# Moving the short convolution of a hybrid decoder block from the attention stage to the gate stage, by way of DRAM

## The chip, the cores and the metric

One Trainium2 chip; the kernel runs on one NeuronCore of it. The metric is the device time of one execution in microseconds. Engines are named as in the profile: PE is TensorE (matmul), PEld its weight loads, DVE is VectorE, ACT is ScalarE, POOL is GpSimd, SP is SyncE, which here issues nearly all DMAs. Each engine works through its own queue in order.

## The reference

One decoder block in float32: 1024 tokens and 16 meta tokens, 1024 channels. The part that matters is the mixer: one input projection gives eight groups of 1024 channels; a short gated convolution and a stick-breaking attention run on them side by side, and two sigmoid gates merge the two.

```python
def hybrid_mixer(xn, w_in, conv_w_mix, w_proj_conv, w_proj_attn, b_gate, w_out):
    h = xn @ w_in
    b_c, c_c, h_c, q, k, v, g_conv, g_attn = jnp.split(h, list(splits), axis=-1)
    y_conv = b_c * causal_dwconv(c_c * h_c, conv_w_mix)      # 3 taps, per channel
    branch_conv = y_conv @ w_proj_conv
    o = stick_breaking_attention(q.reshape(hd), k.reshape(hd), v.reshape(hd))
    branch_attn = o.reshape(bsz, seq_len, D_ATTN) @ w_proj_attn
    gate_conv = jax.nn.sigmoid(g_conv + b_gate[0])
    gate_attn = jax.nn.sigmoid(g_attn + b_gate[1])
    merged = gate_conv * branch_conv + gate_attn * branch_attn
    return merged @ w_out
```

After it come a residual with RMSNorm, a gated MLP with a convolution of its own, and a second residual.

## The kernel before

Activations lie transposed, channels on the 128 partitions and positions along the free axis. 1026 positions are worked on (`NQ`), in three chunks of 342 (`CH`). To keep float32 precision, each operand of a product is split into a high and a low part of type float32r: ScalarE casts the high part, VectorE (or GpSimd, for weights) subtracts it from the value to get the low part. The helper `split` does this (L64, L65). Each product is then three matmuls: high by high, high by low, low by high (L124 to L126).

**Dense items.** A list of items holds the input projection, one item for each block of 128 output channels. An item is three chunks of 24 matmuls each (8 blocks of input channels, three matmuls each) into one of three PSUM buffers (`ps_mm`), and after each chunk a function of the item, `evac`, takes the result out of PSUM. The class `Dense` runs them step by step, one step being three matmuls; `chunk()` runs eight steps. At an item's start the weights of the next are split (`whi` by ScalarE, `wlo` by GpSimd, 2 buffers each) and those of the one after are loaded (`raw`, 2 buffers, L100).

**Attention stage.** For 8 pairs of heads, two streams of attention work, `stage1` (scores, sigmoids, a scan along the keys on VectorE, products on GpSimd) and `stage2` (transposes into PSUM, split into `ah` and `al`, products with the values), are interleaved with dense steps by a planner that weighs costs written in the code. For each pair the dense items are: v, q and k of the next pair, the three items of one convolution block (`items_conv`: c, h and b) and one gate (four with the last pair). The convolution block works so: `evac_c` copies c out of PSUM (ScalarE, L272), `evac_h` multiplies it by h (VectorE, L276), and after the third chunk of h `conv3` runs on the whole block of 1026 positions: one tap on ScalarE (L196), two on VectorE (L197, L198). `evac_b` multiplies by b (VectorE, L283), and the result goes to the DRAM tensor `y_d` (L285). The tiles of this work (`cc`, `yy`, the gates' `gt`, `vt`, `ot`) share four buffers of the tag `wk`.

**Gate stage.** When the attention work is through, the gate items that are left run alone on TensorE. The buffers of the attention stage are given up and reused: `yT` (three tiles, one for each chunk of positions, high and low) lies there, and the pool `sw` with two buffers a tag. In this loop `load_split` loads a block of `y_d` into `ld` (L553) and splits it into `yT`; it is called once ahead of each of the first eight chunks.

**After it.** `item_pc` multiplies `yT` by `w_proj_conv` (8 items; each chunk reads all eight blocks of `yT`), takes in the gate `gcl` (L594) and stores `m_d`; meanwhile `o_d` is split into `oT`. `item_pa` does the same for attention and adds the two (L615). Then come the output projection, the norms and the MLP.

The framework puts the instructions of each engine into an order of its own, from the program's order as priority and its own estimate of when an instruction can start; so a load or a cast can stand ahead of instructions that the program names earlier. Semaphores are placed by it too.

Of the kernel before, what the change touches and what calls it, by code (L numbers as in the profile page):

```python
# [8 lines left out]
F32 = mybir.dt.float32  # L9
F32R = mybir.dt.float32r  # L10
AF = mybir.ActivationFunctionType
ALU = mybir.AluOpType
PSUM = bass.MemoryType.PSUM

P = 128
D = 1024
KB = D // P
NMETA = 16
T0 = 14
NT = 1040  # L20
NQ = NT - T0
CH = NQ // 3
# [10 lines left out]
def block_kernel(ctx, tc, x, meta_tokens, g_pre_mix, w_in, channels, w_proj_conv,  # L33
                 w_proj_attn, w_out, g_post_mix, g_pre_ffn, w_up_gate, w_down,
                 g_post_ffn, out):
    nc = tc.nc

    def pool(name, bufs=1, side="left", space=None):
        kw = dict(name=name, bufs=bufs, reuse_waits="tile")
        if space is not None:  # L40
            kw["space"] = space
        else:
            kw["side"] = side
        return tc.tile_pool(**kw)
# [6 lines left out]
    par = const.tile([P, 106], F32, name="par")  # L51

    o_d = tc.dram_tile([D, NQ], F32, name="o_d")
    y_d = tc.dram_tile([D, NQ], F32, name="y_d")
    gc_d = tc.dram_tile([D, NQ], F32, name="gc_d")
    ga_d = tc.dram_tile([D, NQ], F32, name="ga_d")
    m_d = tc.dram_tile([D, NQ], F32, name="m_d")
# [5 lines left out]
    def split(hi, lo, src, lo_engine=None):  # L63
        nc.scalar.copy(hi, src)  # L64
        (lo_engine or nc.vector).tensor_tensor(lo, src, hi.bitcast(F32), op=ALU.subtract)  # L65
# [89 lines left out]
    def col_block(w, c):  # L155
        return w[c]
# [28 lines left out]
    work = at_ctx.enter_context(pool("work", 2, "right"))  # L185
    def w_mix(k, b):
        return par[:, k * 8 + b:k * 8 + b + 1]
# [7 lines left out]
    def conv3(dst, src, n, wt):  # L195
        nc.scalar.activation(dst, src[:, 2:2 + n], AF.Copy, scale=wt(2))  # L196
        nc.vector.scalar_tensor_tensor(dst, src[:, 1:1 + n], wt(1), dst, op0=ALU.mult, op1=ALU.add)  # L197
        nc.vector.scalar_tensor_tensor(dst, src[:, 0:n], wt(0), dst, op0=ALU.mult, op1=ALU.add)  # L198
# [67 lines left out]
    def items_conv(cb):  # L266
        st = {}

        def evac_c(ci, a, n, ps):
            if ci == 0:  # L270
                st["c"] = work.tile([P, NT], F32, name="cc", tag="wk", bufs=4)
            nc.scalar.copy(st["c"][:, a - 12:a - 12 + n], ps)  # L272

        def evac_h(ci, a, n, ps):
            c = st["c"][:, a - 12:a - 12 + n]
            nc.vector.tensor_tensor(c, c, ps, op=ALU.mult)  # L276
            if ci == 2:
                st["y"] = work.tile([P, NT], F32, name="yy", tag="wk", bufs=4)
                conv3(st["y"][:, :NQ], st["c"], NQ, lambda k: w_mix(k, cb))

        def evac_b(ci, a, n, ps):
            y = st["y"][:, a - T0:a - T0 + n]
            nc.vector.tensor_tensor(y, y, ps, op=ALU.mult)  # L283
            if ci == 2:
                nc.sync.dma_start(y_d[cb * P:(cb + 1) * P, :], st["y"][:, :NQ])  # L285

        return [(col_block(w_in, 8 + cb), src_x, CH_C, evac_c),
                (col_block(w_in, 16 + cb), src_x, CH_C, evac_h),
                (col_block(w_in, cb), src_x, CH_Q, evac_b)]
# [121 lines left out]
    n_gates = len(items)  # L411
    dense = Dense(ps_mm, items)
# [132 lines left out]
    sw = s_ctx.enter_context(pool("sw", 2, "right"))  # L545
    gp["p"], gp["n"] = sw, 2

    def slot_tile(pl, name):
        return pl.tile([P, 2, KB, CH], F32R, name=name, tag="t")

    def load_split(tiles, src_d, kb):
        raw = sw.tile([P, NT], F32, name="ld", tag="ld")
        nc.sync.dma_start(raw[:, :NQ], src_d[kb * P:(kb + 1) * P, :])  # L553
        for c in range(3):
            split(tiles[c][:, 0, kb, :], tiles[c][:, 1, kb, :], raw[:, c * CH:(c + 1) * CH])

    yT = [slot_tile(pl, "yT") for pl in (slotA, slotB, slotC)]
    k = 0
    for _ in range(3 * (n_gates - dense.i)):
        if k < 8:  # L560
            load_split(yT, y_d, k)
            k += 1
        dense.chunk()
    while k < 8:
        load_split(yT, y_d, k)
        k += 1

    xnt_ctx.close()
# [60 lines left out]
    k = 0  # L629
# [67 lines left out]
    def out_products(b, c):  # L697
        n = min(CH, D - c * CH)
        ps = ps_o.tile([P, 512], F32, name="po", tag="po")[:QB, :n]
        m = mb[b]  # L700
        for kb in range(KB):
            mh, ml = m[:, 0, kb, :], m[:, 1, kb, :]
            wh, wl = w_o[c][:, 0, kb, :n], w_o[c][:, 1, kb, :n]
            nc.tensor.matmul(ps, mh, wh, start=(kb == 0), stop=False)
            nc.tensor.matmul(ps, ml, wh, start=False, stop=False)
            nc.tensor.matmul(ps, mh, wl, start=False, stop=(kb == KB - 1))
        return ps
# [253 lines left out]
    for b in range(9):  # L961
# [3 lines left out]
        for c in range(3):  # L965
            ps = out_products(b, c)
# [156 lines left out]
    for gi, fbs in enumerate(groups):  # L1123
# [14 lines left out]
        for tb in range(8):  # L1138
# [3 lines left out]
            for hf in range(2):  # L1142
                ps = bank()
                c = slice(hf * 512, (hf + 1) * 512)
# [6 lines left out]
                a = accs[tb][:, c]  # L1151
# [10 lines left out]
            if last:  # L1162
                a, hb, s0 = accs[tb], hbs[tb], ssqs[tb]
                nc.vector.tensor_tensor(s0[:, 0:1], s0[:, 0:1], s0[:, 1:2], op=ALU.add)
                r = rstd_of(fsml, s0[:, 0:1], P)
                for hf in range(2):
                    c = slice(hf * 512, (hf + 1) * 512)
# [60 lines left out]
```

## Time and profile before

| what | value |
|---|---|
| median of 3 runs | 2078.82 us (2075.2 to 2084.7) |
| the profiled execution's own time | 2078.02 us |
| its span in the profile | 2076.3 us |
| TensorE busy | 1990.4 us (96%) |
| VectorE busy | 1069.5 us (52%) |
| ScalarE busy | 850.8 us (41%) |
| GpSimd busy | 902.0 us (43%) |
| DMA | 177.58 MB, mean 86 GB/s |

The attention stage lasts until about 1012 us of the span (its last value product starts at 1011.24), the gate stage until 1058 us, the projections until about 1250 us; the rest is the output projection, the norms and the MLP. Matmul durations overlap each other in the trace, so the pace of TensorE is read from start to start. A row of the timeline gives the start, the duration, the engine, the line and the tiles, and in brackets how long the engine was idle before it and what ended that.

### The profile page before, as it was taken

Reading aid. Unit: us, or ns where it says so; the run is one execution under the profiler, and the core shown is the slowest. Engines: PE = TensorE matmul, PEld = TensorE weight load, DVE = VectorE, ACT = ScalarE, POOL = GpSimd, SP = SyncE. Lnnn points to the kernel's source line nnn. Section 1 sums busy time; section 2 is a strip of 40 time slices with the busy share of each in tenths; the row PEclk is TensorE's granted clock in tenths of the full one; section 3 lists DMA queues with packets and bytes.
Section 4 is the critical chain, followed back from the end, with each engine's and each line's share of the span. In section 5 each row is a group of like instructions: output and inputs, shape, how many; then the busy total and the mean of one; then the engine's idle time right before and its main releaser. Section 6 shows DMA issues by size and latency. Waiting matters only on the chain.

```text
span 2076.3 us, 30859 instructions
## 1 busy us (share of the span) xinstructions
PE 1990.4 (96%) x12228; PEld 1862.1 (90%) x12228; DVE 1069.5 (52%) x1689; ACT 850.8 (41%) x1771; POOL 902.0 (43%) x764
## 2 busy tenths in 40 slices
PE   5999999999999999999999989979999999999997
PEld 5999999999999999999999989968898899878886
DVE  6455565655555565654341115785444444445546
ACT  4444454545454454544341113354334434421122
POOL 4343444434443444444222551225655556555353
PEclk9999999999999999999999999989999999999999
DMA  3111101111111101111475664313222122253323
GB/s 134 42 51 42 61 32 51 42 51 41 52 51 42 52 31 54 49 42 61 141 225 173 177 193 136 96 44 102 76 88 82 62 102 70 74 182 103 100 81 132
DMA packets 56030, 177.58 MB, mean 86 GB/s; under 512 B 12728, under 2 KB 12728, under 8 KB 55884
## 3 DMA queue, kind: packets, MB, share of 16 engines
q1 hardware_dynamic: 54732, 173.50, 25.9%
q8 instruction: 96, 1.57, 0.3%
q10 hardware_dynamic: 1152, 2.10, 0.3%
q14 instruction: 50, 0.41, 0.1%
HBM read 131.36 MB, written 44.21 MB: 85 GB/s over the span
## 4 chain that ended last, share of the span: by engine, by line
PE 78%; DVE 9%; DMA 4%; ACT 3%; POOL 2%; issue 2%; DVEq 0%; SPq 0%; ACTq 0%; POOLq 0%
PE mm L124 13%; PE mm L125 12%; PE mm L126 12%; PE st L858 6%; PE st L862 6%; PE st L860 6%; PE st L1150 3%; PE tp L372 3%; PE st L1148 3%; PE st L1149 3%; PE av L362 2%; PE av L363 2%; PE z L326 2%; PE z L325 2%; POOL a_op L65 1%
## 5 line engine op out<-in xcount | busy, mean ns | idle before, releaser
L124 PE MATMUL mm<-xnT,whi 128*128 128x342 f32 (+2 forms) x1536 | 506.9, 330 | 3.6 <-ACT xnT L64 3.6
L125 PE MATMUL mm<-xnT,whi 128*128 128x342 f32 (+2 forms) x1536 | 495.0, 322 | 0.5 <-DVE xnT L65 0.5
L126 PE MATMUL mm<-xnT,wlo 128*128 128x342 f32 (+2 forms) x1536 | 492.0, 320 | 0.0
L338 POOL TENSOR_TENSOR be<-be,fl 114x127 f32<-114x127 f32 (+2 forms) x144 | 176.8, 1228 | 402.7 <-DVE fl L336 185.8
L124 PEld LDWEIGHTS mm<-xnT,whi 128*128 128x128 f32 x1536 | 291.0, 190 | 8.4 <-ACT xnT L64 4.2
L125 PEld LDWEIGHTS mm<-xnT,whi 128*128 128x128 f32 x1536 | 291.5, 190 | 2.2 <-DVE xnT L65 1.0
L126 PEld LDWEIGHTS mm<-xnT,wlo 128*128 128x128 f32 x1536 | 290.6, 189 | 0.0
L65 POOL TENSOR_TENSOR wlo<-raw,whi 128x1024 fp32r<-128x1024 f32 x80 | 205.7, 2572 | 188.0 <-ACT whi L64 188.0
L65 POOL TENSOR_TENSOR a_op<-raw,a_op 128x512 fp32r<-128x512 f32 (+1 forms) x136 | 191.7, 1422 | 94.4 <-ACT a_op L64 74.1
L336 DVE TENSOR_TENSOR_SCAN fl<-fl 114x128 f32<-114x128 f32 (+2 forms) x144 | 204.9, 1423 | 4.9
L65 DVE TENSOR_TENSOR al<-tp,ah 128x342 fp32r<-128x342 f32 (+4 forms) x288 | 127.0, 450 | 139.5 <-ACT ah L64 137.3
L64 ACT CAST ah<-tp 128x342 fp32r<-128x342 f32 (+4 forms) x288 | 112.8, 398 | 189.8 <-PE tp L372 181.5
L858 PE MATMUL st<-opT,a_op 128*128 128x258 f32 (+2 forms) x528 | 173.1, 328 | 3.4 <-ACT snap L873 1.7
L860 PE MATMUL st<-opT,a_op 128*128 128x258 f32 (+2 forms) x528 | 170.6, 323 | 1.7 <-DVE opT L65 1.7
L862 PE MATMUL st<-opT,a_op 128*128 128x258 f32 (+2 forms) x528 | 170.4, 323 | 0.0
L327 ACT ACTIVATE fl<-z 114x348 f32<-114x348 f32 (+10 forms) x240 | 111.4, 464 | 129.8 <-PE z L326 122.5
L64 ACT CAST a_op<-raw 128x512 fp32r<-128x512 f32 (+1 forms) x136 | 85.0, 633 | 152.4 <-DMA raw<-in_w_up_gate_dram 50.4
L1155 DVE TENSOR_TENSOR acc<-acc,st 128x512 f32<-128x512 f32 x144 | 98.5, 687 | 91.2 <-PE st L1150 91.2
L372 PE MATMUL tp<-ident,be 114*128 114x114 f32 x720 | 119.5, 263 | 25.5 <-DVE al L65 21.1
L858 PE MATMUL st<-opB,a_op 128*128 128x512 f32 (+2 forms) x396 | 127.9, 323 | 0.0
L860 PE MATMUL st<-opB,a_op 128*128 128x512 f32 (+2 forms) x396 | 127.8, 323 | 0.0
L862 PE MATMUL st<-opB,a_op 128*128 128x512 f32 (+2 forms) x396 | 127.3, 322 | 0.0
(172 smaller groups left out, 4367.3 us busy)
## 6 DMA issues: line engine op xcount, KB each, us to landing
raw<-in_w_in_dram SPq DMA_DIRECT2D x64, 512.0 KB
raw<-in_w_up_gate_dram SPq DMA_DIRECT2D x44, 512.0 KB
act_d<-owork SPq DMA_DIRECT2D x22, 512.0 KB
araw<-act_d SPq DMA_DIRECT2D x22, 512.0 KB
raw<-in_w_down_dram SPq DMA_DIRECT2D x22, 512.0 KB
y_d<-yy SPq DMA_DIRECT2D x8, 513.0 KB
ga_d<-gt SPq DMA_DIRECT2D x8, 513.0 KB
o_d<-ot SPq DMA_DIRECT2D x8, 513.0 KB
```

The costliest lines, as they stand in the source:

```text
L64: nc.scalar.copy(hi, src)
L65: (lo_engine or nc.vector).tensor_tensor(lo, src, hi.bitcast(F32), op=ALU.subtract)
L124: nc.tensor.matmul(ps, wh, xh, start=(kb == 0), stop=False)
L125: nc.tensor.matmul(ps, wh, xl, start=False, stop=False)
L126: nc.tensor.matmul(ps, wl, xh, start=False, stop=(kb == KB - 1))
L327: nc.scalar.activation(fl[:, c0:c0 + n], z, AF.Sigmoid, scale=-0.125)
L336: nc.vector.tensor_tensor_scan(fl[:, :nk][:, ::-1], fl[:, :nk][:, ::-1], fl[:, :nk][:, ::-1], 1.0, op0=ALU.mult, op1=ALU.min)
L338: nc.gpsimd.tensor_tensor(be[:, 0:nk - 1], be[:, 0:nk - 1], fl[:, 1:nk], op=ALU.mult)
L372: nc.tensor.transpose(tp[:n, QB * j:QB * (j + 1)], blocks[j][0][:, kb * P:kb * P + n], ident[:QB, :QB])
L858: nc.tensor.matmul(ps, wt[:, 0, k], xh, start=start and kb == 0, stop=False, skip_group_check=True)
L860: nc.tensor.matmul(ps, wt[:, 0, k], xl, start=False, stop=False, skip_group_check=True)
L862: nc.tensor.matmul(ps, wt[:, 1, k], xh, start=False, stop=stop and kb == 3, skip_group_check=True)
```

## The change

In the attention stage `evac_h` no longer runs the convolution: after the third chunk it stores the product c*h (1028 positions, two of them ahead for the taps) to a DRAM tensor `ch_d`. `evac_b` copies b out of PSUM on ScalarE into a tile of its own, and the block is stored to `b_d`. `y_d` is gone.

In the gate stage `conv_split` takes the place of `load_split` for `yT`: it loads a block of `ch_d` (tag `ld`, two buffers) and one of `b_d` (tag `lb`, two buffers), runs `conv3` into `yy` (tag `ly`, one buffer), multiplies by b on VectorE over 1026 positions, and splits the three chunks. The eight calls are spread over the loop instead of standing at its first eight chunks.

```diff
-    y_d = tc.dram_tile([D, NQ], F32, name="y_d")
+    ch_d = tc.dram_tile([D, NQ + 2], F32, name="ch_d")
+    b_d = tc.dram_tile([D, NQ], F32, name="b_d")
...
             if ci == 2:
-                st["y"] = work.tile([P, NT], F32, name="yy", tag="wk", bufs=4)
-                conv3(st["y"][:, :NQ], st["c"], NQ, lambda k: w_mix(k, cb))
+                nc.sync.dma_start(ch_d[cb * P:(cb + 1) * P, :], st["c"][:, :NQ + 2])
 
         def evac_b(ci, a, n, ps):
-            y = st["y"][:, a - T0:a - T0 + n]
-            nc.vector.tensor_tensor(y, y, ps, op=ALU.mult)
+            if ci == 0:
+                st["b"] = work.tile([P, NT], F32, name="bb", tag="wk", bufs=4)
+            nc.scalar.copy(st["b"][:, a - T0:a - T0 + n], ps)
             if ci == 2:
-                nc.sync.dma_start(y_d[cb * P:(cb + 1) * P, :], st["y"][:, :NQ])
+                nc.sync.dma_start(b_d[cb * P:(cb + 1) * P, :], st["b"][:, :NQ])
...
+    def conv_split(cb):
+        ch = sw.tile([P, NT], F32, name="ch", tag="ld")[:, :NQ + 2]
+        bv = sw.tile([P, NT], F32, name="bv", tag="lb")[:, :NQ]
+        nc.sync.dma_start(ch, ch_d[cb * P:(cb + 1) * P, :])
+        nc.sync.dma_start(bv, b_d[cb * P:(cb + 1) * P, :])
+        y = sw.tile([P, NT], F32, name="yy", tag="ly", bufs=1)[:, :NQ]
+        conv3(y, ch, NQ, lambda k: w_mix(k, cb))
+        nc.vector.tensor_tensor(y, y, bv, op=ALU.mult)
+        for c in range(3):
+            split(yT[c][:, 0, cb, :], yT[c][:, 1, cb, :], y[:, c * CH:(c + 1) * CH])
+
+    chunks = 3 * (n_gates - dense.i)
     k = 0
-    for _ in range(3 * (n_gates - dense.i)):
-        if k < 8:
-            load_split(yT, y_d, k)
+    for i in range(chunks):
+        if k < 8 and i >= k * (chunks - 2) // 8:
+            conv_split(k)
             k += 1
         dense.chunk()
     while k < 8:
-        load_split(yT, y_d, k)
+        conv_split(k)
         k += 1
```

## The prediction

> **What bounds the kernel now.** I read the shares of the page first, then TensorE's waits in the attention stage, then the chain of work around one such wait, then the same place in order of time, and last the gate stage that the convolution moves into.
>
> ```profile
> PE 1990.4 (96%) x12228; PEld 1862.1 (90%) x12228; DVE 1069.5 (52%) x1689; ACT 850.8 (41%) x1771; POOL 902.0 (43%) x764
> ```
>
> TensorE is busy 96% of the span, so all that can be won is its idle time, and a new idle time costs its full length. Its waits between 60 and 960 us (attention), then three pieces of the chain of work near 331 us (start, length, what):
>
> ```profile
> PE tp L372 <- DVE al L65: 18.6, 17, 1.6
> PE tp L372 <- DVE vv L65: 4.3, 6, 0.7
> ...
> 331.27 0.93 issue
> 332.20 1.16 ACT yy L196
> ...
> 333.39 3.19 DVE yy L197
> ```
>
> The largest wait is for VectorE's `al` split, 18.6 us in 17 waits, and the chain into one of them runs through the convolution: ScalarE's tap (L196), then VectorE's second tap (L197). In order of time:
>
> ```profile
> 333.11 2.39 POOL L65 TENSOR_TENSOR wlo<-raw,whi 128x1024 fp32r<-128x1024 f32 x1
> 333.39 3.19 DVE L197 SCALAR_TENSOR_TENSOR yy<-cc,par,yy 128x1026 f32<-128x1026 f32 x1 [1.47 <-ACT yy L196]
> 335.17 0.32 PE L124 MATMUL mm<-xnT,whi 128*128 128x342 f32 x1
> 336.50 0.50 DVE L65 TENSOR_TENSOR al<-tp,ah 128x342 fp32r<-128x342 f32 x1
> 337.06 0.30 PE L372 MATMUL tp<-ident,be 114*100 114x114 f32 x1 [1.57 <-DVE al L65]
> ```
>
> `al` sits behind L197 on VectorE's queue. L197 takes 3.19 us because GpSimd's weight split `wlo` started 0.28 us earlier; it ends 1.07 us after `wlo`. TensorE starts its last matmul at 335.17 and its next at 337.06. The instructions of the tile `yy` (min/median/max ns), and ScalarE's PSUM copy of the c product:
>
> ```profile
> L283 DVE TENSOR_TENSOR yy<-yy,mm x24: 478/480/511, 111.2 to 927.4; 128x342 f32<-128x342 f32 x24
> L196 ACT ACTIVATE yy<-cc,par x8: 1146/1152/1154, 105.5 to 911.1; 128x1026 f32<-128x1026 f32 x8
> L197 DVE SCALAR_TENSOR_TENSOR yy<-cc,par,yy x8: 2764/3197/3210, 106.7 to 912.3; 128x1026 f32<-128x1026 f32 x8
> L198 DVE SCALAR_TENSOR_TENSOR yy<-cc,par,yy x8: 1272/1272/1278, 109.6 to 915.8; 128x1026 f32<-128x1026 f32 x8
> L272 ACT COPY cc<-mm x24: 433/446/455, 81.6 to 894.3; 128x342 f32<-128x342 f32 x16, 128x344 f32<-128x344 f32 x8
> ```
>
> It happens eight times, once a pair. L198 is the same operation without a `wlo` beside it: 1.27 us, so the collision costs 1.93 us.
>
> Three rows of TensorE at full pace, and two stretches, one of attention and one of the gate stage (busy us and count of PE, its weight loads, DVE, ACT and POOL; granted clock; DMA share; GB/s):
>
> ```profile
> 1057.15 0.32 PE L124 MATMUL mm<-xnT,whi 128*128 128x342 f32 x1
> 1057.31 0.32 PE L125 MATMUL mm<-xnT,whi 128*128 128x342 f32 x1
> 1057.46 0.31 PE L126 MATMUL mm<-xnT,wlo 128*128 128x342 f32 x1
> ...
> 400.00:600.00 200.00, 195.23 (x1277) 188.11 (x1276) 118.94 (x186) 100.16 (x230) 89.59 (x99) 1.00 0.14 48
> 1017.00:1062.00 45.00, 45.00 (x289) 45.00 (x288) 12.27 (x25) 21.37 (x46) 9.44 (x5) 1.00 0.77 221
> ```
>
> A matmul of 342 columns starts every 0.157 us.
>
> **Part 1: what the attention stage gains.** Removed from VectorE per block: 3.20 + 1.27 + 3 x 0.48 = 5.9 us; from ScalarE 1.15. Added to ScalarE: three copies of b, by the c copy's row 3 x 0.446 = 1.34 us. So ScalarE stays level (+0.19 us a block) and VectorE loses 47 us in all. What counts is TensorE: at full pace the matmul after 335.17 would start at 335.33, so one stall is 1.73 us, eight are 13.8. Smaller slips around it (products waiting for the same `al`) I estimate at 0.2 us a block. Without L196 ahead of it `ah` is cast a microsecond sooner, `al` follows at once, and I see nothing late next. The gain lies between 8 x 1.57 = 12.6 (the idle alone) and 18.6 (every wait for `al`, though some fall elsewhere); I take 15.5, nearest to the eight stalls.
>
> The added copies cost nothing while a PSUM buffer is spare (three); without that cover, at most 24 x 0.446 = 10.7 us. They stand where the c copies stand, at which TensorE shows no wait, so zero. The store of `ch_d` waits for the third L276 product, earlier than the old `y_d` store waited for L283; behind it on SyncE's queue stand weight loads needed a whole item later. `b_d` replaces `y_d` one for one. Eight more stores of about 513 KB meet a DMA system 14% busy in this stage: zero. `cc` is held until its store lands instead of until L198; with four buffers, zero.
>
> **Part 2: what the gate stage must now do.** Between the last attention product and the first matmul on `yT`, TensorE runs remaining gate products. The rows: SyncE's loads, ScalarE's hi casts, VectorE's lo subtractions, then the matmuls on `yT`.
>
> ```profile
> 1017.43 9.33 SPq L553 DMA_DIRECT2D ld<-y_d  x4
> 1023.26 2.49 ACT L64 CAST yT<-ld 128x342 fp32r<-128x342 f32 x6 [1.58 <-DMA ld<-y_d]
> 1029.37 1.24 ACT L64 CAST yT<-ld 128x342 fp32r<-128x342 f32 x3 [2.23 <-DMA ld<-y_d]
> 1029.88 1.37 DVE L65 TENSOR_TENSOR yT<-ld,yT 128x342 fp32r<-128x342 f32 x3 [3.46 <-ACT yT L64]
> ...
> L124 PE MATMUL mm<-yT,whi x192: 317/318/327, 1058.6 to 1148.3; 128*128 128x342 f32 x192
> ```
>
> The first block arrives at 1023.26, 5.83 us after its load was issued at 1017.43; the tiles overlay attention's buffers and its load stands behind other work of SyncE's queue, so I see no earlier start. `yT` is first read at 1058.6; the eighth block is read after 7 x 3 matmuls of 0.157 us, at 1061.9. That is the deadline.
>
> Now one block of the new `conv_split`. Its tile `yy` (tag `ly`) has one buffer, so a block's first tap cannot start before the last subtraction of the block before has read it. The blocks therefore run in series: ScalarE's tap 1.15, two VectorE taps at 1.27 each, the product with b, and the split, from the first cast (1029.37) to the end of the last subtraction (1029.88 + 1.37 = 1031.25), 1.88. The product of 1026 columns from two SBUF operands has no row; the nearest are L198, as long, at 1.27, and this one:
>
> ```profile
> L65 DVE TENSOR_TENSOR mb<-mraw,mb 128x912 fp32r<-128x912 f32 x4 | 4.4, 1108 | 2.9 <-ACT mb L64 2.6
> ...
> L65 DVE TENSOR_TENSOR oT<-ld,oT x24: 501/509/2449, 1060.5 to 1090.1; 128x342 fp32r<-128x342 f32 x24
> ```
>
> I take 1.27 (1.11 is the low end). One block: 1.15 + 3 x 1.27 + 1.88 = 6.84 us. Seven blocks after 1023.26 bring the eighth to 1071.1; its first third is ready 1.15 + 3.81 + 0.51 (first cast) + 0.51 (first subtraction) = 5.98 later, at 1077.1. That is 15.2 us past the deadline, with no disturbance at all. The placing of the eight calls over the chunks doesn't matter: the last call comes some eleven chunks of 24 x 0.157 = 3.8 us into the stage, before this series reaches it.
>
> Disturbances: weight splits on GpSimd and gate work on ScalarE, between 1026 and 1060 (windows with the tile `whi`, which counts `whi` casts and `wlo` splits, then with `gt`):
>
> ```profile
> 1026.00:1060.00 34.00, 34.00 (x146) 24.93 (x146) 3.84 (x4) 7.42 (x4) 1.00 0.82 233
> 1026.00:1060.00 34.00, 5.16 (x10) 1.00 0.82 233
> ```
>
> Four `wlo` splits fall into the series. Each can hold up a VectorE instruction by 1.93 us (L197 above; the one `oT` subtraction of 2.449 us against 0.509 shows 1.94). VectorE works 3.81 + 1.37 of each 6.84 us, 76%, so I take 4 x 1.93 x 0.76 = 5.9 us, between 0 and 7.7. ScalarE has 3.84 + 5.16 = 9.0 us of casts and sigmoids to place; the series uses ScalarE 2.4 us in 6.84 (35%), so I take 2.5 us, between 0 and 9.0. Ready at about 1085.5: TensorE waits 23.6 us. The gate products' own evacuations can slip behind blocked casts too, but such a slip ends before the series does and costs nothing more.
>
> [...]
>
> After an idle stretch TensorE restarts slowly. Its wait of 4.4 us in the later projection, and the 4 us after it (granted clock is the number after the busy times):
>
> ```profile
> PE mm L124 <- DVE gal L615: 4.4, 1, 4.4
> ...
> 1240.00:1244.00 4.00, 4.00 (x18) 4.00 (x17) 0.81 (x3) 0.48 (x2) 3.35 (x4) 0.61 0.62 179
> ```
>
> A clock of 0.61 over 4 us loses 1.6 us, once, when `yT` is complete.
>
> After that `oT` is split some 25 us later than now; it was done by 1090 and is needed after 1148.3, so 58 us cover it. The queues past which the loads move (SyncE) now carry two loads a block; each waits for its buffer, a weight load behind it by up to a block (6.84 us), inside the 11.3 us of an item of 72 matmuls.
>
> **The sum.** Gain 15.5; new wait 23.6 + 1.6 = 25.2; net +9.7. The profiled execution took 2078.02 us (its span 2076.3), 0.8 below the median of the runs, 2078.82. So 2078.0 + 9.7 = about 2088 us. With bare ends: wait 15.2 to 32 (all disturbances: 15.2 + 7.7 + 9.0), plus 1.6, less 18.6 to 12.6, gives -1.8 to +21: 2076 to 2099.
>
> **Rivals.**
> First, hidden after all, the other side: if the blocks come before 1061.9, only the gain is left, 2078 - 15.5 = 2062.5. It would need a block in (1061.9 - 1023.26 - 5.98)/7 = 4.7 us or a start 15 us sooner with no disturbance; from 4.7 us a block on, each tenth costs 0.7 us. For it: VectorE is busy only 12.3 of 45 us there now. Against it: the series above. Chance 8%.
>
> Second, the bare series, without disturbances, or DMA in its place. The gate stage's row shows 221 GB/s at a 0.77 share between 1017 and 1062. That is 9.9 MB; eight more loads make 14.1, and at 221/0.77 = 287 GB/s they take 49 us, till 1066; with the last block's 6 us behind them, 1072, sooner than the series. So the series binds: 15.2 + 1.6 - 15.5 = +1.3, 2079. Chance 24% for 2073 to 2083.
>
> Third, the stall in attention stays (another instruction ahead of `al`), or a blocked head of ScalarE's queue stretches the series to all its ends: 2078 + 25.2 = 2103, or 2099. Against it: with L196 and L197 gone I see only shorter work ahead of `al` in these rows. Chance 16%.
>
> Fourth, the forecast itself, 2083 to 2095: 52%.
>
> [...]
>
> **How the numbers follow.** A difference of 0.5% is 10.4 us, about what a measurement of this kernel can tell from none: below 2068.4 faster, above 2089.2 slower. The forecast's case lies across that upper bound, some 24 points below and 28 above, since its disturbances have more room upward; with the second rival's 24 below and the third's 16 above: faster 0.08, same 0.48, slower 0.44. The likeliest case's own range is 2083 to 2095; for eight in ten I take 2073 to 2104: below lies the first rival and a little more, above the third at its worst.
>
> **What would show it.** Right: no TensorE wait on `al` of 1.6 us at the pair period; L197 at 1.27 mostly; ScalarE's tap on `yy` every 7 to 8 us from about 1008 on (all shifted by the gain); TensorE waiting on `yT` for some 24 us in pieces, one for each late `kb`, with a lowered clock just after. Wrong: `yT` complete before TensorE asks for it, or VectorE starting one block before the block ahead is split, or the wait on `al` still there with another instruction in front.

## The result, and the profile after

The changed kernel took 2106.41 us (median of 4 runs, 2099.84 to 2107.54) beside 2079.65 for the kernel before on the same chip: ratio 1.0132 [1.0106, 1.0159], 1.3% slower, 2.4 us above the forecast's range. The profiled execution took 2106.9 us (span 2105.2), 28.9 more than the 2078.02 of before.

The first line of the page of after, the shares of busy time:

```profile
PE 1997.5 (95%) x12228; PEld 1869.2 (89%) x12228; DVE 1081.5 (51%) x1673; ACT 860.6 (41%) x1795; POOL 898.2 (43%) x764
```

It shows next to nothing: every share within a point of before. The time has to be looked for by stage. The stage boundaries are starts of TensorE's matmuls (score products, value products, first product with `yT`, with `oT`, with `w_o`), as the group rows of after give them, in the column "first and last start":

```profile
L326 PE MATMUL z<-kk,qh x240: 221/323/424, 75.4 to 998.8; 128*114 128x348 f32 x24, 128*114 128x292 f32 x16, 128*114 128x406 f32 x16, 128*114 128x128 f32 x8
L363 PE MATMUL av<-ah,vv x288: 216/402/635, 90.7 to 1023.8; 128*128 128x342 f32 x96, 100*128 100x114 f32 x16, 58*128 58x114 f32 x16, 128*128 128x228 f32 x16
L125 PE MATMUL mm<-yT,whi x192: 317/318/652, 1075.9 to 1182.3; 128*128 128x342 f32 x192
L125 PE MATMUL mm<-oT,whi x192: 312/320/426, 1182.8 to 1274.3; 128*128 128x342 f32 x192
```

The same cuts for all kernels of this study, in us of one profiled execution each (attention ends with the start of the last value product of either kind, 0.1 us after the row's; the kernels are explained below):

| kernel | start | attention | gate | product with yT | product with oT | rest | span |
|---|---|---|---|---|---|---|---|
| before | 74.7 | 936.6 | 47.3 | 90.2 | 99.9 | 827.7 | 2076.3 |
| before, once more | 76.3 | 935.3 | 47.3 | 90.2 | 99.9 | 829.4 | 2078.4 |
| **after** | 75.4 | 948.5 | 52.0 | 106.9 | 92.0 | 830.4 | 2105.2 |
| after, b copied by VectorE | 75.0 | 938.1 | 51.8 | 106.9 | 92.3 | 831.1 | 2095.1 |
| after, no convolution at all | 75.3 | 944.1 | 47.3 | 92.7 | 91.4 | 829.8 | 2080.5 |
| before, taps left out | 74.7 | 941.3 | 47.3 | 90.2 | 92.2 | 828.6 | 2074.4 |
| before, ScalarE copy added | 75.1 | 964.5 | 47.3 | 90.2 | 93.1 | 825.5 | 2095.7 |
| after, v's wlo on VectorE | 74.4 | 937.1 | 51.8 | 107.3 | 91.8 | 828.8 | 2091.3 |
| after, two yy buffers | 75.7 | 948.9 | 50.7 | 103.8 | 92.0 | 831.5 | 2102.7 |
| after, both of these | 75.6 | 938.6 | 51.0 | 103.5 | 90.9 | 827.2 | 2086.9 |
| after, wlo in quarters | 74.8 | 932.1 | 47.5 | 108.4 | 94.8 | 828.1 | 2085.7 |
| before, wlo in quarters | 73.7 | 927.2 | 47.3 | 90.2 | 99.6 | 830.0 | 2068.0 |
| after, quarters, two yy buffers | 72.4 | 933.6 | 52.5 | 103.5 | 96.8 | 828.9 | 2087.7 |
| the same, b copied by VectorE | 73.8 | 928.3 | 54.5 | 103.6 | 95.9 | 831.7 | 2087.7 |

So of the 28.9 us: attention +11.9 (the forecast had -15.5), gate stage and product with `yT` together +21.4 (forecast +25.2), product with `oT` -7.9 (not forecast), rest and start +3.4.

**Attention.** TensorE's waits of after between 60 and 960 us (us in total, times, longest), the rows that answer to 18.6 and 4.3 of before:

```profile
PE tp L373 <- DVE al L66: 25.8, 23, 2.2
PE tp L373 <- DVE vv L66: 4.3, 6, 0.7
```

The wait for `al` did not go; it grew. Where the taps had been, in order of time, after:

```profile
334.93 1.61 DVE L337 TENSOR_TENSOR_SCAN fl<-fl 114x698 f32<-114x698 f32 x1
335.00 3.71 POOL L66 TENSOR_TENSOR wlo<-raw,whi 128x1024 fp32r<-128x1024 f32 x1
336.46 0.79 DVE L66 TENSOR_TENSOR al<-tp,ah 128x342 fp32r<-128x342 f32 x2
337.00 0.30 PE L373 MATMUL tp<-ident,be 114*100 114x114 f32 x1 [0.61 <-DVE al L66]
```

In the taps' place ahead of `al` stands the next scan of the attention stage, 1.61 us, so TensorE still waits 0.61 instead of 1.57. This time the scan starts 0.07 us ahead of `wlo`, and it is `wlo` that grows (3.71 for 2.4), which hurts nobody. The larger part comes some 20 us (a sixth of a pair) later, at a place that before passes without a gap. There VectorE prepares the tile `fl`, which holds the sigmoids, by a short maximum (L335 of before, L336 of after) and then runs the scan over it; GpSimd's select on `be` and its `wlo` stand beside these. Before, in order of time:

```profile
466.40 0.28 DVE L335 TENSOR_TENSOR fl<-fl,ones_up 114x114 f32<-114x114 f32 x1 [1.62 <-POOL be L338]
466.43 0.40 POOL L339 TENSOR_SCALAR_AFFINE_SELECT be<-be 114x114 f32<-114x114 f32 x1
466.72 2.33 DVE L336 TENSOR_TENSOR_SCAN fl<-fl 114x1040 f32<-114x1040 f32 x1
466.80 4.45 POOL L65 TENSOR_TENSOR wlo<-raw,whi 128x1024 fp32r<-128x1024 f32 x1
468.96 0.91 DVE L65 TENSOR_TENSOR al<-tp,ah 128x342 fp32r<-128x342 f32 x2
```

And after:

```profile
468.21 0.43 ACT L284 COPY bb<-mm 128x342 f32<-128x342 f32 x1
469.23 0.47 ACT L328 ACTIVATE fl<-z 114x344 f32<-114x344 f32 x1
469.47 0.28 POOL L340 TENSOR_SCALAR_AFFINE_SELECT be<-be 114x114 f32<-114x114 f32 x1
469.72 2.38 POOL L66 TENSOR_TENSOR wlo<-raw,whi 128x1024 fp32r<-128x1024 f32 x1
469.81 2.42 DVE L336 TENSOR_TENSOR fl<-fl,ones_up 114x114 f32<-114x114 f32 x1 [2.39 <-POOL be L340]
472.26 2.32 DVE L337 TENSOR_TENSOR_SCAN fl<-fl 114x1040 f32<-114x1040 f32 x1
475.05 0.51 PE L373 MATMUL tp<-ident,be 114*128 114x114 f32 x3 [2.19 <-DVE al L66]
```

Before, the scan starts 0.08 us ahead of `wlo`: GpSimd is held (4.45 us), VectorE is not. After, `wlo` starts 0.09 us ahead of the small operation on `fl` (L336): that takes 2.42 us instead of 0.28, the scan and `al` behind it come 2.1 us late, and TensorE waits 2.19. Such a gap, 2.17 to 2.24 us long, stands in each pair from the second on.

The gaps are only a part of the 11.9 us. TensorE's idle time in the attention stage (the stage less its busy time) is 34.1 us for 26.8 in before, so +7.3. The rest comes from the clock. Five stretches of 3.41 us at half clock, 0.50, stand in the stage in after, four of them at gaps of this kind, and one in before; each loses 1.7 us, so +6.8. The first of them:

```profile
238.20:241.60 3.40, 3.39 (x14) 3.34 (x15) 0.91 (x3) 0.89 (x2) 1.99 (x2) 0.50 0.05 18
```

What is left of the stage without both, 905.8 us for 908.0, hardly differs: it lies between 905.8 and 908.8 us in every profile of the table.

**Gate stage.** The instructions of `yy` and `yT` in after (min/median/max ns, first and last start):

```profile
L65 ACT CAST yT<-yy x24: 470/475/481, 1043.6 to 1100.1; 128x342 fp32r<-128x342 f32 x24
L197 ACT ACTIVATE yy<-ch,par x8: 1152/1154/1159, 1036.4 to 1093.7; 128x1026 f32<-128x1026 f32 x8
L199 DVE SCALAR_TENSOR_TENSOR yy<-ch,par,yy x8: 1282/1290/3306, 1039.0 to 1096.5; 128x1026 f32<-128x1026 f32 x8
L567 DVE TENSOR_TENSOR yy<-yy,bv x8: 1222/1229/3311, 1042.3 to 1098.1; 128x1026 f32<-128x1026 f32 x8
```

ScalarE's tap comes every (1093.7 - 1036.4)/7 = 8.2 us; the last casts end after 1100, and the first product with `yT` stands at 1075.9. Two of L199 and two of L567 take 3.25 to 3.31 us instead of 1.29 and 1.23, each beside a `wlo`. TensorE's waits of after between 1055 and 1110 us:

```profile
PE mm L125 <- ACT yT L65: 11.8, 3, 5.6
PE mm L125 <- ACT gt L299: 2.8, 1, 2.8
```

Two stretches at the end of that wait, with the granted clock (the number after the busy times):

```profile
1090.00:1098.00 8.00, 3.06 (x16) 2.21 (x15) 6.20 (x9) 3.51 (x7) 0.00 (x0) 1.00 0.37 130
1098.00:1104.00 6.00, 4.11 (x13) 3.85 (x14) 5.70 (x12) 3.52 (x7) 0.00 (x0) 0.53 0.58 178
```

TensorE is busy 3.06 of 8 us while it waits for the last blocks, and restarts at a clock of 0.53. In the gate stage and the product with `yT` together, 14.6 us of the 21.4 are idle time and 6.8 are lost at half clock (3.41 us from 1071.1, 3.41 from 1084.7 and 6.83 from 1098.4). Before the last of these waits TensorE has started 63 matmuls on `yT`: the framework put the first seven blocks of all three chunks ahead of the eighth block.

### The profile page after: what moved, and what is told of

Read it like the earlier page. It is cut to its first block, busy times and chain, and to the rows that moved or that the text cites. A ratio compares the mean times of both kernels' runs of the same rounds, so it can differ in the third digit from the quotient of the medians.

```text
span 2105.2 us, 30901 instructions
## 1 busy us (share of the span) xinstructions
PE 1997.5 (95%) x12228; PEld 1869.2 (89%) x12228; DVE 1081.5 (51%) x1673; ACT 860.6 (41%) x1795; POOL 898.2 (43%) x764
## 3 DMA queue, kind: packets, MB, share of 16 engines
q8 instruction: 96, 1.57, 0.3%
## 4 chain that ended last, share of the span: by engine, by line
PE 73%; DVE 13%; ACT 4%; DMA 3%; POOL 3%; issue 2%; DVEq 0%; SPq 0%; POOLq 0%; ACTq 0%
PE mm L125 11%; PE mm L126 11%; PE mm L127 11%; PE st L872 5%; PE st L876 5%; PE st L874 5%; PE st L1164 3%; PE st L1162 3%; PE st L1163 3%; PE tp L373 3%; DVE fl L337 3%; PE av L363 2%; PE av L364 2%; DVE fl L336 2%; POOL a_op L66 2%
## 5 line engine op out<-in xcount | busy, mean ns | idle before, releaser
L336 DVE TENSOR_TENSOR fl<-fl,ones_up 114x114 f32<-114x114 f32 x144 | 71.9, 499 | 127.5 <-ACT fl L328 104.4
L373 PEld LDWEIGHTS tp<-ident,be 114*128 114x128 f32 x720 | 90.5, 140 | 48.9 <-DVE al L66 38.8
L872 PE MATMUL st<-opB,a_op 128*128 128x512 f32 (+2 forms) x396 | 127.5, 322 | 0.0
```

The source lines that it names most:

```text
L336: nc.vector.tensor_tensor(fl[:, nk - QB:nk], fl[:, nk - QB:nk], ones_up, op=ALU.max)
L373: nc.tensor.transpose(tp[:n, QB * j:QB * (j + 1)], blocks[j][0][:, kb * P:kb * P + n], ident[:QB, :QB])
L872: nc.tensor.matmul(ps, wt[:, 0, k], xh, start=start and kb == 0, stop=False, skip_group_check=True)
```

## The experiments

Ratios are to the kernel before, run on the same chip. The theory at this point: in attention it isn't the amount of VectorE's work that counts but who starts first, VectorE or GpSimd's `wlo`, at two places of each pair; taking the taps out and putting copies on ScalarE both shift those starts. The rival: the added copies on ScalarE cost by their own time.

**b copied by VectorE.** In the changed kernel:

```diff
-            nc.scalar.copy(st["b"][:, a - T0:a - T0 + n], ps)
+            nc.vector.tensor_copy(st["b"][:, a - T0:a - T0 + n], ps)
```

> The changed kernel with one edit: b is copied out of PSUM by VectorE, not by ScalarE. Theory A: the attention stage got 12 us longer because the added ScalarE copy of b stands ahead of the sigmoid that the scan waits for, so that VectorE's max (ahead of the scan) starts just after GpSimd's weight split and is blocked by it: the 2.2 us waits on al behind the scan vanish, the attention stage shortens by 18 to 28 us, time 2078 to 2088 us. Theory B: taking the taps away moves the scan under the weight split by itself: the waits stay, time 2101 to 2107 us. The gate stage stays as it is by both.

Measured 2096.58 us, ratio 1.0103 [1.0069, 1.0136]: between the two. Attention falls by 10.4 us to 938.1, yet gaps of 1.87 to 1.97 us stay at the scan of six pairs. Of the 10.4 us, 3.9 are idle time, 6.8 are four stretches at half clock fewer, and what is left of the stage is 0.4 longer. As the next run shows, like gaps do not lower the clock equally often. So ScalarE's copies carry some 4 us here, at most about 10, and are not all of it: without them attention is still 1.5 us above before, not 15 below.

**The convolution left out of the gate stage.** `conv_split` of the changed kernel only loads `ch` and `bv` and splits thirds of them into `yT`; taps and product with b are left out.

> The changed kernel without the convolution in the gate stage: both stores and both loads stay, the three taps and the product with b are left out, and the loaded tiles are split as they are. Both theories: the attention stage stays 12 us longer than in the kernel before; the projection on yT starts and runs without waiting, which takes back the 21 us that the gate stage and the first projection gained, so 2083 to 2087 us. If the loads alone held yT up, it stays above 2095 us.

Measured 2085.43 us, ratio 1.0053 [1.0035, 1.0072], as expected. The gate stage is back at 47.3, the product with `yT` at 92.7: the convolution's series accounts for 18.9 of the 21.4 us. Without it the changed kernel is still no faster than before, so attention has a loss of its own. Attention, in which nothing is edited, has the same seven gaps and the same 34.1 us of idle time as in after, yet takes 944.1 us, not 948.5: only two stretches at half clock stand in it, not five. Stage lengths of single executions differ by a few us for this alone.

**Only the taps taken out.** The kernel before, with the convolution left out (h*c goes on to the product with b as it is):

```diff
-                st["y"] = work.tile([P, NT], F32, name="yy", tag="wk", bufs=4)
-                conv3(st["y"][:, :NQ], st["c"], NQ, lambda k: w_mix(k, cb))
+                st["y"] = st["c"]
```

> The kernel before with the three taps left out: b is multiplied into c*h in place, nothing else changes, nothing moves to the gate stage and ScalarE gets no copy of b. Theory A: the stall behind the taps goes and no other comes: 2062 to 2068 us. Theory B: the scan falls under the weight split as in the changed kernel: 2085 to 2095 us. What I predicted for the attention stage, 15.5 us of gain, would be 2064 us.

Measured 2079.9 us, ratio 1.0033 [1.0011, 1.0055]: neither theory's range, and the forecast's gain of 15.5 us is not there though nothing is added anywhere. Attention takes 941.3, 4.7 more than before; 3.4 of that are idle time, 3.4 half clock, and what is left of the stage is 2.1 shorter. The place of the scan, in this kernel (L334 and L335 are before's L335 and L336):

```profile
465.23 0.28 POOL L338 TENSOR_SCALAR_AFFINE_SELECT be<-be 114x114 f32<-114x114 f32 x1
465.31 0.33 DVE L334 TENSOR_TENSOR fl<-fl,ones_up 114x114 f32<-114x114 f32 x1 [1.63 <-ACT fl L326]
465.48 2.41 POOL L65 TENSOR_TENSOR wlo<-raw,whi 128x1024 fp32r<-128x1024 f32 x1
465.67 4.39 DVE L335 TENSOR_TENSOR_SCAN fl<-fl 114x1040 f32<-114x1040 f32 x1
```

In before, the operation on `fl` starts 0.03 us ahead of GpSimd's select, here 0.08 us behind it. So `wlo`, which follows the select, starts 0.19 us ahead of the scan instead of 0.08 behind, and the scan takes 4.39 us instead of 2.33. A tenth of a microsecond turns a hidden collision into one on the path.

**Only the copies added.** The kernel before, taps kept, with a copy of the same shape on ScalarE in `evac_b` (its result is not used):

```diff
+            nc.scalar.copy(st["c"][:, a - T0:a - T0 + n], ps)
```

> The kernel before with one instruction more per chunk: ScalarE copies b out of PSUM into the block's c tile, which nobody reads after that; VectorE's product with b stays. Theory A: the added copy delays the sigmoid, the max falls behind the weight split: waits of about 2.2 us appear beside the old ones, 2090 to 2100 us. Theory B: ScalarE has room for 24 copies of 0.45 us: 2078 to 2082 us.

Measured 2099.13 us, ratio 1.0115 [1.0078, 1.0153], as theory A said. TensorE's wait for `al` in attention:

```profile
PE tp L373 <- DVE al L65: 31.8, 23, 2.3
```

Attention takes 964.5 us: copies of 24 x 0.446 = 10.7 us by their own time cost 27.9. The old stall (some 2.25 us in each pair, counted from TensorE's starts against their usual pitch) stays, and the scan's collision comes on top: 15.5 us of the 27.9 are idle time, nearly all of it seven new gaps of 2.17 to 2.26 us, and 12.0 are half clock. The copies here are not quite those of the changed kernel: VectorE's product with b waited for them 16 times, 14.4 us in all. Next to this kernel the changed one, with no taps, is 16.0 us shorter in attention. That this comes near the forecast's 15.5 for the taps is partly luck: 8.2 of the 16.0 are idle time, 5.2 half clock. The old stall is a real cost where the collision at the scan is there anyway, but against the kernel before, which did not have that collision, the 15.5 is wrong.

**The kernel before once more,** unchanged:

> The kernel before, unchanged, on the chip that the next kernels run on. It tells what two executions of one program differ by in each stage. In the first profiles the second projection took 100.1 us in the kernel before and 92.1 us in the changed one, though nothing of the change runs in it. If the change did that, this profile shows about 100 us again; if it differs from execution to execution, about 92 us. The attention stage should take 936 us again (first score product to last value product).

Attention 935.3 and product with `oT` 99.9 again, in a total of 2080.09 us: these stage lengths repeat and belong to the program. Its attention is 1.3 us shorter and has no stretch at half clock, where the first profile has one.

**Other owner for the colliding split.** In the changed kernel, the `wlo` of the seven v items, the one that meets the scan, moves to VectorE:

```diff
-                split(hi, lo, raw, nc.gpsimd)
+                split(hi, lo, raw, nc.vector if i in self.on_dve else nc.gpsimd)
```

> The changed kernel with the low weight part of seven items (the v item that follows each gate) subtracted by VectorE instead of GpSimd; the order of TensorE's, ScalarE's and SyncE's queues stays the same. Theory: the gain of the attention stage is lost to one collision a pair, where this weight split on GpSimd starts just ahead of VectorE's max and scan and blocks them for 2.1 us. With the split on VectorE there is no second engine to block: the 2.2 us waits after b's last chunk go, the attention stage falls from 948 to 920 to 928 us, time 2080 to 2088 us (ratio 1.000 to 1.005). Rival: the waits come from the taps' removal in the order of the queues, not from the collision; then VectorE's added 1.2 us makes it equal or slower, ratio 1.012 to 1.018.

Measured 2093.39 us, ratio 1.0078 [1.0053, 1.0103]; less gain than expected. Attention falls by 11.4 us to 937.1. The 2.2 us gap is gone from most pairs, though up to 1 us stays there, since these seven splits now stand on VectorE's own queue and take 2.07 us on average. Two long gaps are left at these places, and both are holds of the same kind: 3.17 us at 680.9, where a `wlo` that is still GpSimd's starts together with the operation on `fl` at 676.26 (2.50 us for 0.28), and 2.18 us at the scan of the last pair, where no v item follows the gate and the split was not moved.

**Two buffers for yy** in the changed kernel (`bv` and `yy` cut to 1026 columns to make room):

```diff
-        y = sw.tile([P, NT], F32, name="yy", tag="ly", bufs=1)[:, :NQ]
+        y = sw.tile([P, NQ], F32, name="yy", tag="ly", bufs=2)
```

> The changed kernel with two buffers for the convolution's tile yy in the gate stage instead of one (and that tile and b's tile shortened to 1026 columns, to make room). Theory: the blocks run in series because of the one buffer, 8.2 us a block with the collisions; with two, VectorE's own 5.2 us a block plus four collisions of 2 us set the pace, the eighth block is ready 11 to 14 us sooner, time 2092 to 2096 us (ratio 1.006 to 1.009). Rival: the loads or VectorE bound it anyway, gain under 4 us, ratio 1.011 or more. The attention stage stays at 948 us by both.

Measured 2098.73 us, ratio 1.0101 [1.0065, 1.0138], between the two. TensorE's waits between 1030 and 1115 us in this kernel:

```profile
PE mm L125 <- ACT yT L65: 7.1, 3, 4.4
PE mm L126 <- DVE yT L66: 1.4, 2, 0.7
```

And its casts (first and last start):

```profile
L65 ACT CAST yT<-yy x24: 462/473/482, 1044.1 to 1090.1; 128x342 fp32r<-128x342 f32 x24
```

The last cast starts 10.0 us sooner than in after, but TensorE gets back 4.4 (50.7 + 103.8 against 52.0 + 106.9): the framework now starts only 23 matmuls on `yT` ahead of the last wait, not 63. The other 40, at 0.157 us some 6.3 us of work that filled the wait in after, come behind it.

**Both edits together:**

> Both edits together: two buffers for yy, and the seven weight splits on VectorE. If the two causes are separate the gains add up: 2106 - 12 - 22 = about 2072 us, ratio 0.995 to 0.999, as fast as the kernel before or a little faster. If they overlap, 1.002 or more.

Measured 2088.99 us, ratio 1.0062 [1.0037, 1.0087]: attention 938.6 and product with `yT` 103.5, so the two gains stand side by side. The ratio is where overlapping gains were expected, because each gain by itself was smaller than assumed.

**`wlo` in quarters.** Four pieces of 256 columns in place of one of 1024, in the changed kernel:

```diff
-                split(hi, lo, raw, nc.gpsimd)
+                nc.scalar.copy(hi, raw)
+                for k in range(0, D, 256):
+                    nc.gpsimd.tensor_tensor(lo[:, k:k + 256], raw[:, k:k + 256],
+                                            hi[:, k:k + 256].bitcast(F32), op=ALU.subtract)
```

> The changed kernel with GpSimd's low part of each attention and gate weight (wlo, 128x1024, 2.35 to 2.40 us) cut into four subtractions of 256 columns, about 0.6 us each; nothing else is edited, though the scheduler is free to place the rest a little differently. Theory A (what stands in TensorE's way twice per pair is one VectorE instruction that may not run beside a wlo that has begun, so it waits for the rest of that one instruction): a wait is now at most one quarter, 0.6 instead of 2.1 us. The 2.2 us gap at the second place of each pair falls below 1 us, attention goes from 948.5 to 933-940 us, and the four collisions among the taps of the gate stage go from 2.0 to at most 0.6 us each, so that the stage loses another 2 to 4 us: ratio to the kernel before 1.002-1.007. Theory B (VectorE and GpSimd share a fixed amount of time, however it is cut): the quarters follow one another without a hole, VectorE waits for all four, and the ratio stays at 1.010-1.014.

Measured 2089.35 us, ratio 1.0090 [1.0061, 1.0119]. Attention falls by 16.4 us to 932.1, a little more than theory A asked for (8.5 less idle time, and with no gap above 1.31 us but the last, no stretch at half clock, another 8.5); gate stage and product with `yT` lose 3.0, as expected; the product with `oT` is 2.8 longer. The ratio is above theory A's range, whose lower attention it has. The place of the scan in this kernel:

```profile
463.61 4.86 POOL L110 TENSOR_TENSOR wlo<-raw,whi 128x256 fp32r<-128x256 f32 x4
463.70 0.78 DVE L336 TENSOR_TENSOR fl<-fl,ones_up 114x114 f32<-114x114 f32 x1 [2.38 <-POOL be L340]
464.52 2.74 DVE L337 TENSOR_TENSOR_SCAN fl<-fl 114x1040 f32<-114x1040 f32 x1
467.72 0.51 PE L373 MATMUL tp<-ident,be 114*128 114x114 f32 x3 [0.97 <-DVE al L66]
```

`wlo` starts 0.09 us ahead of the operation on `fl`, just as in after. But this now waits for one quarter (0.78 us for 2.42), the scan loses 0.4, GpSimd's third piece waits for the scan, and TensorE's gap is 0.97 instead of 2.19 us. Same order, same lead, only a shorter instruction in front: the hold falls from 2.14 us (2.42 - 0.28) to 0.50 (0.78 - 0.28). The span is 19.5 us (0.9%) shorter than after's, the ratio only 0.4% lower; the two ratios come from different chips, each with an interval of 0.3% to either side.

The same cut in the **kernel before**:

> The kernel before with the same cut of wlo into quarters. Theory A: the two taps that run beside a wlo in each pair of the kernel before lose at most 0.6 instead of 1.2 to 2.0 us, the 2.25 us gap of TensorE there falls to 1-1.5 us, and attention goes from 936.6 to 925-931 us: ratio 0.993-0.998. Theory B: no change, 0.999-1.002. If the second place (max and scan), which the kernel before passes by 0.08 us, tips here as it did without the taps, theory A says that it costs less than 0.7 us per pair, so the sign stays.

Measured 2068.61 us, ratio 0.9976 [0.9961, 0.9992]: inside what was expected, and the only version here that is faster than before, by 0.24%. Its second tap:

```profile
L197 DVE SCALAR_TENSOR_TENSOR yy<-cc,par,yy x8: 1304/1548/1807, 106.0 to 903.5; 128x1026 f32<-128x1026 f32 x8
```

And its wait for `al` in attention:

```profile
PE tp L372 <- DVE al L65: 11.4, 11, 2.4
```

L197 at 1.55 instead of 3.20 us, the wait at 11.4 instead of 18.6, attention 9.4 us shorter: one line takes away most of the stall out of which the change moves the taps, with no price in the gate stage.

**Quarters and two yy buffers** in the changed kernel:

> The changed kernel with wlo in quarters and two buffers for yy, so that the copy scaled by the third tap no longer waits for the three splits of the block before. Theory A: the gain of the quarters and the 4 us that the second buffer brought by itself add up: ratio 0.999-1.004. Theory B: the second buffer alone, 1.008-1.011.

Measured 2087.48 us, ratio 1.0078 [1.0058, 1.0099], where theory A said at most 1.004: the gains did not add up. Against the quarters alone the product with `yT` lost 4.9, but the gate stage (52.5) and the product with `oT` (96.8) gave 7.0 back. In the gate stage 4.8 us of that are a wait of 3.1 for the gate's `gt` and one stretch at half clock; the rest was not followed. Finally **the same with b copied by VectorE** (its expectation calls the 2.14 us hold by an uncut `wlo` the long lock):

> The changed kernel with wlo in quarters, two buffers for yy, and b copied out of PSUM by VectorE instead of ScalarE: all three edits that helped. What it tells: with the long lock gone, what are the two halves of the change worth in attention? Theory A (once a blocked instruction waits for one quarter only, the taps cost TensorE nothing in attention, as the trace of the kernel before with quarters shows, where the 1.6 us gap is gone; so there is no longer anything to win there by taking them out): attention comes to 926-932 us, as in the kernel before with quarters (927.0) and no lower, the 14 to 18 us of waiting in the gate stage stay, the second projection gives back 3 to 8, and the ratio is 1.000-1.006: slower than the kernel before with quarters (0.9976). Theory B (the forecast's own: less work on VectorE in attention is worth some 15 us once the collision is out of the way): attention 912-920 us, ratio 0.994-0.999.

Measured 2081.85 us, ratio 1.0045 [1.0026, 1.0063] (its profiled execution, 2089.58, is the longest of its runs). Attention is 928.3, level with the 927.2 of before with quarters: with `wlo` in quarters, taking the taps out of attention wins nothing, and the cost of the gate stage is all that is left of the change. Theory A.

## Why the prediction was wrong, point by point

- **Gain in attention, forecast -15.5 (bounds 12.6 to 18.6): measured +11.9. This is the step that failed,** at "I see nothing late next" and at the bounds, which allowed no loss. The reading of the stall was right (a tap held by `wlo`, in each pair; beside `wlo` in quarters it takes 1.55 us instead of 3.20). But 0.9 of the 2.25 us stays, because the framework puts the next scan ahead of `al`; and the scan's place 20 us on tips into a collision of the same kind. The taps' removal by itself turns the gain into +4.7. The sum also had no term for the clock in attention, and 6.8 of the 11.9 us are lost there at half clock.
- **ScalarE's copies at zero (at most 10.7):** failed as well. Alone they cost 27.9 us in the kernel before (15.5 idle, 12.0 half clock); in the changed one, moving them to VectorE wins 10.4 (3.9 idle, 6.8 half clock). In the rows above a copy of 0.43 us stands ahead of the `fl` that the scan waits for, with 0.08 us of lead to lose.
- **The new wait, forecast 25.2 with the lowered clock: 21.4.** Right in mechanism; that the size is near is luck, since two errors cancel. The idle time is 14.6 us, not 23.6: the forecast let 21 matmuls on `yT` stand ahead of the eighth block, and the framework put 63 there, which fills some 6.6 us of the wait. Half clock costs 6.8 us, not 1.6. The series itself was well read. From the first tap to the first third of the eighth block, high and low, it was 62.2 us by the forecast (1085.5 - 1023.26) and is 64.0 (1036.41 to 1100.39, where the last block's first subtraction ends). Four collisions cost 2.02, 2.08, 2.08 and 1.96, together 8.1 us, where 5.9 was taken and 7.7 was the upper end. The product with b took 1.23 us, 1.27 was taken. The rows of attention above show as long a hold: L336 took 2.14 us more (2.42 for 0.28) beside a `wlo` of 2.38 that had begun 0.09 us earlier, nearly all of the 2.29 us that were left of it.
- **The restart at a low clock:** there, 0.53 over 6 us, but not once, "when `yT` is complete": three stretches, 6.8 us for the 1.6 that was taken.
- **Load start, SyncE's queue, the placing of the calls at no cost:** right; the first load is issued 6.2 us after the last value product in both kernels (1030.14 and 1017.43).
- **The product with `oT`, not in the sum: -7.9.** Before has there a wait of 4.4 us for `gal` and three for `wlo`, 2.4 us together. After has only this between 1185 and 1300 us:

```profile
PE mm L125 <- DVE gal L629: 0.9, 1, 0.9
```

The two kernels with edits in attention alone also have 92 to 93 us there, with the same order of instructions in that stage as before, and only the loads landing differently: in before the last load of `w_out` takes 6.8 us (issued 1227.13), without the taps 3.3. Before with quarters, the other kernel with a long stage (99.6), has 6.5 there. What makes the load slow was not tried; this part stays open, as do the 3.4 us in start and rest, which lie inside what these columns vary by among the kernels.

The account: 9.7 + 27.4 (attention) - 3.8 (wait) - 7.9 + 3.4 = 28.8, measured 28.9. The third rival (a stall stays, with another instruction ahead of `al`; 2099 to 2103, 16%) came nearest, though it knew neither the place nor that the stall could be more than before. The forecast called "the wait on `al` still there with another instruction in front" the sign of its being wrong, and so it is.

## What to carry to other kernels

A stall read in the trace is a gain only if the queue behind the removed instruction holds nothing as long; look at what the framework will put there, and at every other place on the path where the same two engines start within some tenths of a microsecond of each other. Where VectorE and GpSimd share work on the path, first cut GpSimd's long instructions into short ones: it takes one line, and in both kernels tried here TensorE's wait for `al` fell (25.8 to 18.4 us in the changed one, 18.6 to 11.4 in the one before), while taking work out, adding copies or moving splits between engines each left or made a collision elsewhere. Price a gap on TensorE twice: by its length, and by the half clock that may follow it (1.7 us for a stretch of 3.41 us at 0.50 here). And give an added instruction on a half-idle engine a price from the lead it takes from what is behind it, not from its length.

## What the runs showed of the hardware

- The order of two starts decided some 2 us in these rows: leads of 0.07 and 0.08 us for VectorE left TensorE without the long wait (`wlo` grew to 3.71 and 4.45), leads of 0.09 and 0.19 us for `wlo` held VectorE for its rest (the operation on `fl` 2.42 us for 0.28, the scan 4.39 for 2.33).
- With `wlo` in four pieces of 256 columns (463.61 in the changed kernel with quarters) the operation on `fl` waits for the first one only (0.78 us), the scan loses 0.4 us to the second, and the third waits for the scan (2.74 us for 0.73).
- `al`, which takes one operand from PSUM, ran beside `wlo` at its usual pace (0.79 us for two, at 336.46); none of the 288 of after took over 0.52 us.
- A gap of 2.2 us was followed by a lowered clock in one place and not in another. After the gaps that end at 356.63 and 475.05 in the changed kernel, of 2.24 and 2.19 us:

```profile
357.00:361.00 4.00, 4.00 (x21) 3.89 (x19) 1.03 (x2) 0.89 (x2) 1.61 (x2) 0.59 0.00 0
475.00:479.00 4.00, 3.95 (x28) 3.91 (x29) 1.84 (x4) 1.24 (x3) 2.15 (x3) 1.00 0.02 5
```

So a collision on the path cost some 2.4 us in one pair (from start to start 472.54 to 475.05, less the usual 0.157) and 4 in another (354.07 to 356.63 less 0.157, and 1.7 at half clock). In after all five stretches at a lowered clock in attention are 3.41 us long at 0.50, and they start whole multiples of 3.41 us apart (238.2, 357.7, 593.2, 944.8 and 982.3). So where a gap falls against such multiples may decide; that is a guess from these five, not tested by itself. Of the seven gaps of 2.17 to 2.24 us at the scan, four were followed by such a stretch in after, two in the same stage of the kernel with no convolution.
